# Memory queries by token halves at the start of layer two, and the first output step of the drain by token tile

## The chip, the cores and the metric

The kernel runs on one core of one Trainium2 chip. A core has five engines that run side by side, each with its own queue of instructions: TensorE (PE, matrix products, with its weight loads shown as PEld), VectorE (DVE), ScalarE (ACT), GpSimd (POOL) and SyncE (SP), which here only issues transfers. Times are microseconds (us) on the device, from the first to the last instruction of one execution and what lies around them; several executions are summed up by their median.

## The reference, cut to what matters

Two layers act on 1024 tokens of width 1024. Each layer projects its input x once into main columns, memory queries and two gates, runs a main branch and a cross-attention into 256 memory tokens, gates both, projects out and normalizes. The change lies where layer two (index 1) begins and where it ends.

```python
def memory_attention(q_mem, mem, w_mem_kv):
    mkv = mem @ w_mem_kv
    mk = mkv[..., :D_MEM].reshape(B, M, MEM_HEADS, MEM_HEAD_DIM)
    mv = mkv[..., D_MEM:].reshape(B, M, MEM_HEADS, MEM_HEAD_DIM)
    q = q_mem.reshape(B, S, MEM_HEADS, MEM_HEAD_DIM)
    logits = jnp.einsum('bshd,bmhd->bhsm', q, mk, ...) * (MEM_HEAD_DIM ** -0.5)
    p = jax.nn.softmax(logits, axis=-1)
    return jnp.einsum('bhsm,bmhd->bshd', p.astype(mv.dtype), mv).reshape(B, S, D_MEM)

def mixer_sublayer(x, mem, w_in, w_mem_kv, w_out, main_fn):
    h = x @ w_in
    ...
    y = jnp.concatenate([y_main * jax.nn.silu(g_main), y_mem * jax.nn.silu(g_mem)], axis=-1)
    return y @ w_out
...
        x = layer_norm(ALPHA * x + y, ln_g[layer], ln_b[layer])
```

D_MEM is 512: four heads of 128. The memory tokens and their keys and values don't depend on x. The memory queries do, and so wait in layer two for the normalized output of layer one.

## The kernel before

**Precision.** Every product is made of three matmuls. An operand is split into a high part (a copy rounded to fp32r, made by ACT at line 187) and a low part (the difference in bf16, made by DVE or POOL at line 188); the products high by high, high by low and low by high are added up in PSUM. `grouped` (line 220) puts the high by high products of a group first, or with `turned` last.

**A slab** (line 231) projects one block of 128 output columns for all 1024 tokens. It loads its weights in two pieces of 128x512 into `raw` (four buffers in a ring), splits each into the rings `w` and `wl` (four buffers each), and then makes two halves of 24 matmuls: first tokens 0 to 511, then tokens 512 to 1023. Each half fills one of the two banks of PSUM named `pj`, and at its end an evacuation empties the bank. The function is a generator: what calls it decides how far it runs. For a memory query the evacuation is one `hi_lo` (line 184), a copy on ACT and a difference on DVE.

**The seam between the layers.** `OutProj.rest` (line 532) ends layer one: for each pair of row tiles (256 tokens) it makes the output projection, and `norm` (line 565) adds the residual and normalizes on DVE with one square root on ACT. A normalized row tile becomes input of layer two in `turned_rows` (line 340): ACT and DVE make two half-precision parts (L344, L345), SP issues two transposing transfers (L347, L348), and ACT, DVE and POOL write the transposed block into the tensors called A (L349, L350, L351). For the last two row tiles (tokens 768 to 1023) this is called from `mem_attention` of layer two, through the list `turns`.

**Layer two begins** with `mem_kv(1)` (line 284), which loads and splits the memory tokens, then `mem_attention` (line 370): the two last row tiles, the four memory keys one after another (`keys`, 24 matmuls of 128x256 each, which need no x), and then the four memory queries as slabs, with the values of a head after each (the first value between the two halves of the first query). The split of a memory weight's first piece is given to POOL (line 301).

**Layer two ends** in `OutProj.early` (line 521), the first output step: product group 2 (the memory heads) for the first pair of row tiles, while the last heads of the main attention still run, pumped in small pieces between them. `open` (line 488) takes its four banks: two named `L` for the first row tile and the two `pj` for the second. `rest` then runs the other steps; that with product group 1 of the first pair needs the output of the last pair of heads, which `pair_out` (line 984) multiplies with its gate on POOL and writes to DRAM.

**What sets the order.** PE runs in the order in which the program is written. The instructions of ACT, DVE, POOL and SP are put in order when the program is built, by a planner that sees the whole program; on the chip each queue runs strictly in that order, so that one waiting instruction holds up all that stand behind it.

Of the kernel before, what the change touches and what calls it, by code (L numbers as in the profile page):

```python
# [9 lines left out]
F32 = mybir.dt.float32  # L10
F32R = mybir.dt.float32r
# [66 lines left out]
def run(units):  # L78
    for _ in units:
        pass  # L80
# [19 lines left out]
def trunk_kernel(ctx, tc, x, xT, memT, win, wk, wv0, wv, wmk, wmv, wout, poolw, pscale, lng, lnb, bforget, out):  # L100
# [25 lines left out]
    def sb(shape, tag, bufs, dt=F32, where=None):  # L126
        return (where or pool).tile(shape, dt, tag=tag, name=nm(tag), bufs=bufs)
# [4 lines left out]
    def G(shape=(P, S), dt=F32):  # L132
        return sb(list(shape), "G", 4, dt)
# [17 lines left out]
    def cut(pair, *key):  # L151

        return type(pair)(t[key] for t in pair)
# [5 lines left out]
    def in_place(make, shape):  # L159

        hi = make(list(shape))
        return hi, InPlace((make(list(shape), BF16), hi.bitcast(BF16)[..., 1::2]))
# [34 lines left out]
        nc.gpsimd.tensor_scalar(hi, src, 1.0, 1.0, ALU.mult, ALU.mult)  # L197
        nc.gpsimd.tensor_tensor(lo[0], src, hi.bitcast(F32), ALU.subtract)  # L198

    def split_w(src_dram, shape, by=nc.vector):  # L200
        r = raw(shape)
        nc.sync.dma_start(r, src_dram)
        h, l = in_place(wt, shape)
        gp_hi_lo(h, l, r) if low[0] else hi_lo(h, l, r, by=by)
        return h, l

# [21 lines left out]
        for i, (a, b) in enumerate(terms):  # L228
            nc.tensor.matmul(acc, a, b, start=i == 0, stop=i == len(terms) - 1)  # L229

    def slab(pieces_dram, XH, XL, evac, banks=("pj", 2)):

        ready = isinstance(pieces_dram, list)
        if ready:
            ws = pieces_dram
        else:
            ws = [split_w(pieces_dram[0], [P, 4, P])]
            yield 0
            ws.append(split_w(pieces_dram[1], [P, 4, P]))
            yield 0  # L240

        def terms(n, kts):
            cols = slice(n * NH, (n + 1) * NH)
            out = []
            for kt in kts:
                h, l = ws[kt // 4]
                out.append(three((h[:, kt % 4, :], cut(l, slice(None), kt % 4)), (XH[:, kt, cols], cut(XL, slice(None), kt, cols))))
            return out

        def put(acc, a, b, start, stop):  # L250
            nc.tensor.matmul(acc, a, b, start=start, stop=stop)  # L251
            since[0] += NH

        if ready:
            accs = [ps([P, NH], *banks) for _ in range(2)]
            for kt in range(KT):
                both = [terms(n, [kt])[0] for n in range(2)]
                for i in range(3):
                    for n in range(2):
                        put(accs[n], *both[n][i], kt == 0 and i == 0, kt == KT - 1 and i == 2)  # L260
                yield 6 * NH
            for n in range(2):
                evac(slice(n * NH, (n + 1) * NH), accs[n])
            return
        for n in range(2):
            acc = ps([P, NH], *banks)
            one, two = (terms(n, range(4 * pc, 4 * pc + 4)) for pc in range(2))
            order = grouped(one) + grouped(two, True) if n == 0 else grouped(two + one)
            if n:
                order = order[:KT] + order[KT + KT :] + order[KT : KT + KT]  # L270
            for j, (a, b) in enumerate(order):
                put(acc, a, b, j == 0, j == len(order) - 1)
                if j == len(order) - 1:
                    evac(slice(n * NH, (n + 1) * NH), acc)
                yield NH
# [93 lines left out]

    def mem_attention(l, XH, XL, kv, qtile, ytile, yd):  # L370

        (kh, kl, v, undo), keys, vals = kv
        qs = []
        if l:
            while turns:
                turns.pop(0)(lambda: vt([P, D], F16), lambda: vt([P, 2 * KT, P], F16))
            for h in range(4):
                keys(h)
        for h in range(MH):
            qh, ql = in_place(qtile, [P, S])  # L380
            units = slab(win[l, 8 + h], XH, XL, lambda cols, acc: hi_lo(qh[:, cols], cut(ql, slice(None), cols), acc))
            if l and not h:
                run(islice(units, 3 * KT + 2))
                vals(0)
            run(units)
            qs.append((qh, ql))
            if not l:
                keys(h)
            if not l or h:
                vals(h)  # L390
        ys, gs = [ytile() for _ in range(MH)], [G() for _ in range(MH)]
        pt, fill = {}, Fill()
        for h in range(MH):
# [58 lines left out]
    class OutProj:  # L452
# [68 lines left out]
        def early(self, y, yh, yl):  # L521


            nc.sync.dma_start(y, self.yd[2, :, :, : 2 * P])
            yield
            for two in (slice(0, 2), slice(2, 4)):
                hi_lo(yh[:, two, :], cut(yl, slice(None), two), y[:, two, :], True)
                yield
            self.accs = self.open(0)
            yield from self.products(self.accs, 2, yh, yl)  # L530

        def rest(self, resid, XH, XL, dst):
            self.split(24)
# [169 lines left out]
    with tc.tile_pool(name="in1", bufs=1) as in1:  # L703
# [7 lines left out]
        def vt(shape, dt=F32R):  # L711
            return sb(shape, "V", 4, dt, in1)

        kv = mem_kv(1)
        with tc.manual_schedule(engines={PE}):
            mem_attention(1, XH, XL, kv, xy, lambda: vt([P, S], F32), y1d[2])
        cumd = dram.tile([HEADS, S], F32, name="cumd")
        fg = G((P, 8, ST * HEADS))
        flog = fg[:, 0, :]
# [444 lines left out]
```

## Time and profile before

| | us |
|---|---|
| median of 3 runs | 1215.21 (1212.19 to 1216.25) |
| the profiled execution | 1217.81, of which its span is 1215.6 |
| PE busy | 1180.0 (97% of the span) |
| DVE busy | 798.4 (66%) |
| ACT busy | 616.6 (51%) |
| POOL busy | 200.4 (16%) |
| PE's last matmul of layer one | ends about 456.4 |
| last token of layer two's input written | 479.6 |
| last matmul | ends 1207.3 |

Times in the trace count from the span's start. A wait row names the waiting engine and line, what released it, and then the total, the number and the longest of such waits. A timeline row has start, duration, engine, line, operation, output and input tiles, and in brackets the idle time before it and what ended it. A row of windows gives, for a stretch, busy time and count of each engine, the granted clock of TensorE, and the share of the DMA engines. Two instructions that follow each other on an engine overlap a little in the records: copies of 128x512 on ACT last 0.62 us each and start 0.52 us apart.

### The profile page before, as it was taken

How to read it: one execution, taken by the hardware profiler on the slowest of the kernel's cores; microseconds unless marked ns; L12 is line 12 of the kernel's file. 1: busy time of each engine (PE TensorE's matmuls, PEld its weight loads, DVE VectorE, ACT ScalarE, POOL GpSimd, SP SyncE). 2: the span in 40 equal slices, each digit the busy share in tenths (PEclk: the TensorE clock that was granted, in tenths of full speed). 3: DMA queues.
4: the chain of work that ended last, by engine and by line, in shares of the span. 5: the costliest groups of instructions: out<-in, count | busy, mean ns of one | idle time of the engine just before them, and what ended most of it. 6: DMA issues, size and time to landing. Idle time of an engine off the chain costs nothing. (4 is left out here: it accounts for less than half of the span.)

```text
span 1215.6 us, 19488 instructions
## 1 busy us (share of the span) xinstructions
PE 1180.0 (97%) x6837; PEld 743.0 (61%) x6954; DVE 798.4 (66%) x1868; ACT 616.6 (51%) x1318; POOL 200.4 (16%) x304
## 2 busy tenths in 40 slices
PE   8999999999999997999999999999999999999997
PEld 4566665555555555666775666666666666655554
DVE  6644767375666657357555878777878878775654
ACT  6433654262522235356333777767766777783110
POOL 2000000000000012100003334333334324530000
PEclk9999999999999999999999999999999999999998
DMA  6333654242445567245527789889897999995431
GB/s 234 108 102 93 133 113 156 78 130 71 142 153 156 156 173 184 77 107 103 175 53 170 158 184 182 177 169 187 176 194 165 196 178 210 235 234 181 167 110 47
DMA packets 284305, 182.83 MB, mean 150 GB/s; under 512 B 229168, under 2 KB 242608, under 8 KB 284208
## 3 DMA queue, kind: packets, MB, share of 16 engines
q1 hardware_dynamic: 284208, 181.59, 61.4%
q8 instruction: 54, 0.88, 0.3%
q14 instruction: 43, 0.35, 0.1%
HBM read 94.97 MB, written 22.61 MB: 97 GB/s over the span
## 5 line engine op out<-in xcount | busy, mean ns | idle before, releaser
L251 PE MATMUL pj<-A,w 128*128 128x512 f32 (+1 forms) x1887 | 600.5, 399 | 3.6 <-ACT A L187 2.2
L251 PE MATMUL pj<-A,wl 128*128 128x512 bf16 x951 | 360.7, 381 | 4.8 <-DVE wl L188 0.6
L251 PEld LDWEIGHTS pj<-A,w 128*128 128x128 f32 x976 | 180.8, 189 | 45.7 <-ACT A L187 3.1
L251 PEld LDWEIGHTS <-w 128*128 128x128 bf16 x992 | 95.8, 98 | 123.3 <-issue 36.0
L251 PEld LDWEIGHTS <-wl 128*128 128x128 bf16 x992 | 97.5, 98 | 95.1 <-issue 5.8
L915 ACT ACTIVATE T<-MK,s 128x512 f32<-128x512 f32 x192 | 111.0, 578 | 58.0 <-DVE s L907 36.7
L937 DVE SCALAR_TENSOR_TENSOR P<-T,s,P 128x512 f16<-128x512 f32 x192 | 111.9, 613 | 31.5 <-ACT P L936 30.0
L936 ACT ACTIVATE P<-T,s 128x512 f16<-128x512 f32 x192 | 102.6, 575 | 48.7 <-issue 27.4
L518 PEld LDWEIGHTS <-T 128*128 128x128 bf16 x736 | 70.6, 98 | 87.3 <-issue 4.4
L188 DVE TENSOR_TENSOR wl<-raw,w 128x512 bf16<-128x512 f32 x98 | 69.2, 712 | 82.8 <-ACT w L187 81.4
L187 ACT CAST w<-raw 128x512 fp32r<-128x512 f32 x106 | 64.8, 617 | 98.5 <-PE pj L251 67.6
L229 PE MATMUL L<-B,B 128*128 128x512 f32 (+3 forms) x384 | 109.9, 389 | 3.2 <-DVE s L907 2.9
L229 PEld LDWEIGHTS L<-B,B 128*128 128x128 f32 x384 | 71.1, 189 | 28.5 <-DVE s L907 9.0
L351 POOL TENSOR_SCALAR A<-A 128x1024 bf16<-128x1024 f32 x8 | 8.4, 1052 | 423.5 <-ACT A L349 423.5
L907 DVE CUSTOM_DVE_ANT_0 MK<-L,R 128x512 f32<-128x512 f32 (+3 forms) x128 | 72.5, 567 | 8.4 <-DMA R<-cumd 5.0
L899 POOL TENSOR_SCALAR_AFFINE_SELECT R<-R 128x128 f32<-128x128 f32 x128 | 41.4, 329 | 207.8 <-DVE s L907 111.5
L198 POOL TENSOR_TENSOR wl<-raw,w 128x512 bf16<-128x512 f32 x54 | 69.1, 1280 | 3.5
L188 DVE TENSOR_TENSOR T<-T,T 128x1024 bf16<-128x1024 f32 x23 | 31.9, 1387 | 50.8 <-ACT T L187 50.7
L187 ACT CAST T<-T 128x1024 fp32r<-128x1024 f32 x23 | 24.1, 1048 | 76.9 <-DMA T<-y1d 50.4
L197 POOL TENSOR_SCALAR w<-raw 128x512 fp32r<-128x512 f32 x54 | 34.3, 634 | 74.8 <-PE pj L251 74.7
L518 PE MATMUL L<-B,T 128*128 128x512 bf16 (+1 forms) x164 | 43.0, 391 | 0.2
L966 PE MATMUL O<-T,V 128*128 128x128 f16 x576 | 38.5, 220 | 4.8 <-DMA T<-P 4.8
(277 smaller groups left out, 1744.1 us busy)
## 6 DMA issues: line engine op xcount, KB each, us to landing
raw<-in_win_dram SPq DMA_DIRECT2D x96, 256.0 KB, 2.9
raw<-in_wout_dram SPq DMA_DIRECT2D x40, 256.0 KB, 2.9
B<-B SPq DMA_DIRECT2D x32, 256.0 KB, 4.9
R<-cumd SPq DMA_DIRECT2D x16, 512.0 KB, 4.5
y0d<-Y SPq DMA_DIRECT2D x12, 512.0 KB, 3.2
T<-y0d SPq DMA_DIRECT2D x12, 512.0 KB, 5.3
T<-y1d SPq DMA_DIRECT2D x11, 512.0 KB, 4.2
raw<-in_wmk_dram SPq DMA_DIRECT2D x16, 256.0 KB, 2.7
```

The costliest lines, as they stand in the source:

```text
L187: pin(nc.scalar.copy(hi, src))
L188: pin(by.tensor_tensor(lo[0], src, hi.bitcast(F32), ALU.subtract))
L198: nc.gpsimd.tensor_tensor(lo[0], src, hi.bitcast(F32), ALU.subtract)
L229: nc.tensor.matmul(acc, a, b, start=i == 0, stop=i == len(terms) - 1)
L251: nc.tensor.matmul(acc, a, b, start=start, stop=stop)
L518: nc.tensor.matmul(acc, y, w, start=c == 2 and j == firsts[id(acc)], stop=c == 1 and j == lasts[id(acc)])
L899: nc.gpsimd.affine_select(R[:, qs], R[:, qs], [[-1, P]], ALU.is_ge, -NEG, base=0, channel_multiplier=1).ins
L907: nc.vector.tensor_tensor_reduce(p[:, lo:up], lg, R[:, lo:up], 1.0, top, ALU.add, ALU.min, m[:, n : n + 1])
L915: nc.scalar.activation(e, p[:, lo:up], AF.Exp, bias=top, scale=-1.0, accum_out=sums[:, n, hd % 2, i : i + 1],)
L936: nc.scalar.activation(pair[:, lo:up], e, AF.Copy, scale=r)
L937: nc.vector.scalar_tensor_tensor(pair[:, L + lo : L + up], e, r, pair[:, lo:up], ALU.mult, ALU.subtract)
L966: nc.tensor.matmul(acc[:, cols(i)], v[:, b, 2 * j : 2 * j + 2, :].rearrange("p e d -> p (e d)"), pt[hd, i][:, j, :], start=n == 0, stop=Fa ...
```

## The change

`split_w` and `slab` take an argument `make` that says where the split weights are kept. In layer two, `mem_attention` now builds the four memory queries first. The weights of the first two go to the rings `w` and `wl`, those of the last two to three buffers of the ring `P`, whose other use at that time is the weights and the two scale rows of layer one's output step. All eight pieces are loaded and split ahead of the last two row tiles; then come the first halves of all four queries; then `mem_kv(1)`, which was called ahead of `mem_attention` before; then the second halves in turn, with keys and values between them. In the drain, `early` orders its matmuls by row tile: all products of the first row tile (two banks), then those of the second with the high products last. The numbers of matmuls, splits and transfers stay as they were.

```diff
-    def split_w(src_dram, shape, by=nc.vector):
+    def split_w(src_dram, shape, by=nc.vector, make=wt):
         r = raw(shape)
         nc.sync.dma_start(r, src_dram)
-        h, l = in_place(wt, shape)
+        h, l = in_place(make, shape)
         gp_hi_lo(h, l, r) if low[0] else hi_lo(h, l, r, by=by)
...
-    def slab(pieces_dram, XH, XL, evac, banks=("pj", 2)):
+    def slab(pieces_dram, XH, XL, evac, banks=("pj", 2), make=wt):
...
-            ws = [split_w(pieces_dram[0], [P, 4, P])]
+            ws = [split_w(pieces_dram[0], [P, 4, P], make=make)]
             yield 0
-            ws.append(split_w(pieces_dram[1], [P, 4, P]))
+            ws.append(split_w(pieces_dram[1], [P, 4, P], make=make))
             yield 0
...
     def mem_attention(l, XH, XL, kv, qtile, ytile, yd):
 
-        (kh, kl, v, undo), keys, vals = kv
-        qs = []
+        qs = [in_place(qtile, [P, S]) for _ in range(MH)] if l else []
+
+        def query_units(h, make):
+            qh, ql = qs[h]
+            return slab(win[l, 8 + h], XH, XL, lambda cols, acc: hi_lo(qh[:, cols], cut(ql, slice(None), cols), acc), make=make)
+
+        def aside_homes():
+
+            lows = sb([P, 4, 4, P], "P", 4, BF16)
+            for n in range(2):
+                highs = sb([P, 2, 4, P], "P", 4, F32R)
+                left = [[highs[:, k], lows[:, 2 * n + k]] for k in range(2)]
+                yield lambda shape, dt=F32R, left=left: left[0].pop(0) if dt == F32R else left.pop(0)[0]
+
         if l:
+            homes = aside_homes()
+            units = [query_units(h, wt if h < 2 else next(homes)) for h in range(MH)]
+            for two in units:
+                run(islice(two, 2))
             while turns:
                 turns.pop(0)(lambda: vt([P, D], F16), lambda: vt([P, 2 * KT, P], F16))
-            for h in range(4):
+            for two in units:
+                run(islice(two, 3 * KT))
+            kv = mem_kv(l)
+        (kh, kl, v, undo), keys, vals = kv
+        for h in range(MH):
+            if l:
+                run(units[h])
+                for what, which in ((), ((keys, 0), (keys, 1)), ((keys, 2), (vals, 0)), ((keys, 3), (vals, 1)))[h]:
+                    what(which)
+            else:
+                qs.append(in_place(qtile, [P, S]))
+                run(query_units(h, wt))
                 keys(h)
-        for h in range(MH):
-            qh, ql = in_place(qtile, [P, S])
-            units = slab(win[l, 8 + h], XH, XL, lambda cols, acc: hi_lo(qh[:, cols], cut(ql, slice(None), cols), acc))
-            if l and not h:
-                run(islice(units, 3 * KT + 2))
-                vals(0)
-            run(units)
-            qs.append((qh, ql))
-            if not l:
-                keys(h)
-            if not l or h:
                 vals(h)
+        if l:
+            vals(2)
+            vals(3)
...
             self.accs = self.open(0)
-            yield from self.products(self.accs, 2, yh, yl)
+            parts = self.terms(self.accs, 2, yh, yl)
+            yield from self.ordered(grouped(parts[0] + parts[1]) + grouped(parts[2] + parts[3], True), 2)
...
-        kv = mem_kv(1)
         with tc.manual_schedule(engines={PE}):
-            mem_attention(1, XH, XL, kv, xy, lambda: vt([P, S], F32), y1d[2])
+            mem_attention(1, XH, XL, None, xy, lambda: vt([P, S], F32), y1d[2])
```

**PE at the seam.** First the order before, from the last matmul of layer one (bank L_3818) on; T are the split memory tokens, A the normalized input, w and wl the split weights.

```order
L518 MATMUL L_3818<-G_3128,T_3877 128x512
L229 LDWEIGHTS w_4104
L229 MATMUL pj_4101<-T_4051,w_4104 128x256
...
L229 MATMUL L_4141<-T_4050,w_4144 128x256 x4
...
L229 MATMUL L_4221<-T_4050,w_4224 128x256 x4
...
L251 MATMUL pj_4275<-A_3059,w_4265 128x512 x4
```

The same place in the changed kernel:

```order
L537 MATMUL L_3818<-G_3128,T_3877 128x512
L251 MATMUL pj_4123<-A_3059,w_4065 128x512 x4
...
L251 MATMUL pj_4150<-A_3059,w_4077 128x512 x4
...
L251 MATMUL pj_4177<-A_3059,P_4061 128x512 x4
...
L251 MATMUL pj_4204<-A_3059,P_4062 128x512 x4
...
L251 MATMUL pj_4260<-A_3059,w_4071 128x512 x4
```

The four keys (pj_4101 to L_4221) stood between layer one and the first product with A; now four half slabs on A, each in a new bank (pj_4123, 4150, 4177, 4204), follow at once, and pj_4260 is the first bank that takes tokens 512 to 1023.

**ACT at the seam, changed kernel**, from the half-precision part of row tile 6 (V_4103) to that of row tile 7 (V_4113) and on; P_4062 are the fourth query's weights, T_4231 and T_4233 memory tokens, B the queries.

```order
L344 ACTIVATE V_4103<-G_3998,unrow 128x1024
L187 CAST T_4231<-raw_4235 128x512
...
L349 ACTIVATE A_3059<-V_4107,unrow 128x8x128
L600 ACTIVATE s_4029<-s_4028 128x1
L187 CAST P_4062<-raw_4095 128x512
...
L187 CAST B_4052<-pj_4123 128x512
L187 CAST T_4233<-raw_4245 128x512
...
L344 ACTIVATE V_4113<-G_4020,unrow 128x1024
L187 CAST B_4054<-pj_4150 128x512
L349 ACTIVATE A_3059<-V_4117,unrow 128x8x128
L187 CAST B_4056<-pj_4177 128x512
```

The evacuations of the first three half slabs (B_4052, B_4054, B_4056) stand behind the row tiles' work on ACT. The order before at that place:

```order
L344 ACTIVATE V_4081<-G_3998,unrow 128x1024
L187 CAST w_4184<-raw_4182 128x512
L580 ACTIVATE s_4029<-s_4028 128x1
L187 CAST MK_4074<-pj_4101 128x256
...
L349 ACTIVATE A_3059<-V_4085,unrow 128x8x128
...
L187 CAST MK_4074<-L_4141 128x256
...
L344 ACTIVATE V_4091<-G_4020,unrow 128x1024
L187 CAST w_4265<-raw_4263 128x512
```

There the key evacuations (MK_4074) and the weights of keys and first query (w) stood between the same steps.

**PE in the drain.** Before, behind the first pieces of `early`; L_12359 is the second bank of the first row tile, pj_12360 and pj_12361 those of the second:

```order
L518 MATMUL L_12359<-V_11821,B_12019 128x512 x2
L518 MATMUL L_12359<-B_12200,B_12019 128x512 x2
L518 MATMUL pj_12360<-B_11717,B_12019 128x512 x2
L518 MATMUL pj_12360<-MK_11904,B_12019 128x512 x2
L518 MATMUL pj_12361<-V_11821,B_12019 128x512 x2
L518 MATMUL pj_12361<-B_12200,B_12019 128x512 x2
```

And in the changed kernel:

```order
L537 MATMUL L_12354<-V_11816,B_12014 128x512 x2
L537 MATMUL L_12354<-B_12195,B_12014 128x512 x2
L537 LDWEIGHTS B_12014
L537 MATMUL L_12353<-B_11713,B_12014 128x512
L537 LDWEIGHTS B_12015
L537 MATMUL L_12353<-B_11713,B_12015 128x512
```

The pj banks no longer come after the eight high products of the first row tile; the 16 small products of that row tile on the two L banks are now ahead of them.

## The prediction

> **What bounds the kernel now.** I read the first part of the page (busy times), then who waited for whom on PE, then the windows and timelines at the two places that the change touches. The page:
>
> ```profile
> PE 1180.0 (97%) x6837; PEld 743.0 (61%) x6954; DVE 798.4 (66%) x1868; ACT 616.6 (51%) x1318; POOL 200.4 (16%) x304
> ```
>
> PE is busy for 1180.0 of 1215.6 us, and the change leaves every matmul in place. So it can win only from the idle 35.6 us of PE, and only from waits that it takes away. PE's waits (total, number, longest):
>
> ```profile
> PE L L229 <- DVE s L907: 2.9, 8, 0.7
> PE pj L229 <- DVE T L188: 2.8, 1, 2.8
> PE pj L518 <- DVE G L282: 1.5, 1, 1.5
> PE pj L229 <- DVE wl L188: 1.1, 2, 0.8
> PE L L229 <- POOL wl L188: 0.9, 1, 0.9
> PE L L518 <- ACT T L187: 0.8, 1, 0.8
> PE pj L251 <- DVE wl L188: 0.6, 1, 0.6
> PE L L229 <- DVE wl L188: 0.4, 1, 0.4
> PE L L229 <- ACT w L187: 0.4, 1, 0.4
> ```
>
> The rows with T, w and wl at L229 and L251 are memory keys, a first value and a first query that wait for their split operands: 2.8 + 1.1 + 0.9 + 0.6 + 0.4 + 0.4 = **6.2 us**. The windows show that all of it lies at the seam:
>
> ```profile
> 456.40:460.10 3.70, 0.99 (x9) 0.73 (x8) 3.70 (x6) 3.60 (x6) 1.95 (x1) 1.00 0.10 18
> 460.10:480.00 19.90, 16.71 (x115) 12.36 (x116) 14.94 (x25) 10.44 (x21) 6.81 (x5) 1.00 0.95 227
> 500.00:530.00 30.00, 29.88 (x172) 19.86 (x173) 13.27 (x31) 9.19 (x16) 2.57 (x2) 1.00 0.29 87
> ```
>
> From 456.4 to 460.1 PE worked 0.99 of 3.70 us, and to 480.0 it worked 16.71 of 19.90; by 500 it is full. DVE and ACT were nearly full in the first stretch: memory splits, key weights and the normalization of the last row tiles shared them. The third row of the waits (1.5) is the second place, the first output step of the drain.
>
> **The change at the seam: what PE gets to do.** Instead of keys, PE now has four half slabs on tokens 0 to 511, which were written long before. Their length comes from the first query's second half, which began at 482.80, and the next half, which followed at 487.92 without a wait:
>
> ```profile
> 482.80 2.00 PE L251 MATMUL pj<-A,w 128*128 128x512 f32 x8
> 487.92 1.52 PE L251 MATMUL pj<-A,w 128*128 128x512 f32 x5
> ```
>
> That is 5.1 us, 5.2 with the change between the two kinds of matmul; four last 20.8 us, from 456.4 to **477.2**. Their weights: the first two loads take the place of the memory loads, whose first copy ran at 446.8, and the rest follow through the ring `raw` at 2.9 us a load:
>
> ```profile
> raw<-in_win_dram SPq DMA_DIRECT2D x96, 256.0 KB, 2.9
> ```
>
> With 0.62 for a copy and 0.68 for a low part, behind tile 6's and tile 7's normalization in DVE's new order, the first query's weights are split by 449, the second's by 456, the third's by 457, each ahead of its half (456.4, 461.6, 466.8).
>
> **What PE then waits for.** At 477.2 it needs tokens 512 to 1023, and so row tile 7. Before, that came so (ACT, DVE, SP, POOL):
>
> ```profile
> 446.82 0.62 ACT L187 CAST T<-raw 128x512 fp32r<-128x512 f32 x1 [1.90 <-DMA raw<-in_memT_dram]
> 459.11 1.15 ACT L344 ACTIVATE V<-G,unrow 128x1024 f16<-128x1024 f32 x1
> 467.44 1.15 ACT L349 ACTIVATE A<-V,unrow 128x1024 fp32r<-128x1024 f16 x1 [1.46 <-DMA V<-V]
> 471.97 1.15 ACT L344 ACTIVATE V<-G,unrow 128x1024 f16<-128x1024 f32 x1 [1.65 <-DVE G L588]
> 477.23 1.15 ACT L349 ACTIVATE A<-V,unrow 128x1024 fp32r<-128x1024 f16 x1 [0.90 <-DMA V<-V]
> 457.13 0.68 DVE L575 SCALAR_TENSOR_TENSOR G<-G,L 128x512 f32<-128x512 f32 x1
> 464.87 0.73 DVE L586 SCALAR_TENSOR_TENSOR G<-G,s,P 128x512 f32<-128x512 f32 x1
> 468.73 3.20 DVE L588 SCALAR_TENSOR_TENSOR G<-G,s,P 128x512 f32<-128x512 f32 x2
> 461.27 1.24 SPq L347 DMA_TRANSPOSE V<-V  x1
> 473.21 1.25 SPq L347 DMA_TRANSPOSE V<-V  x1
> 469.69 1.69 POOL L188 TENSOR_TENSOR wl<-raw,w 128x512 bf16<-128x512 f32 x1
> 478.46 1.10 POOL L351 TENSOR_SCALAR A<-A 128x1024 bf16<-128x1024 f32 x1 [1.07 <-ACT A L349]
> ```
>
> The first transfer of row tile 6 left at 461.27 and its user began at 467.44 (6.2 us); that of row tile 7 left at 473.21, its user at 477.23 (4.0). I step through the new order of ACT, DVE and SP with both prices, which are the ends of this unknown:
>
> 1. ACT's query weights are copied by about 453, so V of tile 6 waits only for layer one's last weights: 456.4, done 457.5; its transfer leaves at 457.6 (3.7 earlier than before) and lands at 461.6 or 463.8.
> 2. ACT then writes A (1.15), takes the square root of tile 7 (0.2), copies the fourth query's weights (two, 1.1) and empties the first query's bank (0.6): 464.6 or 466.8. DVE's part of that bank, behind two low parts, ends near 465.9 or 467.8. The third half slab takes this bank at 466.8: a wait of 0 or 1.0.
> 3. DVE scales tile 7 (L588, two halves at 0.73): 467.3 or 469.2. Before, it ended at 471.9, with 3.20 for the two, while POOL split a key weight (469.69, 1.69) beside it. That POOL work is now later.
> 4. The last memory pieces load behind the fourth query's low parts (+2.9), four copies follow on ACT (2.1), then V of tile 7 (1.15): done at 470.6 or 472.6. This, not the scaling, is what is late next. The second query's bank is emptied behind it, at 472.5 or 474.5; the fourth half, due at 472.0, waits 0.5 or 2.5.
> 5. The transfer takes 4.0 or 6.2, A 1.15: 475.8 or 480.0 (478.4 before).
>
> These waits do not add up to more than the last of them: PE goes on with the second halves at the later of the fourth half's end (472.5 or 474.5, plus 5.2, so 477.7 or 479.7) and the arrival of the third bank and of the tokens (about 476.5, or 481.0 with DVE's part of that bank). Against 477.2 it has lost **0.5 or 3.8**. I take 1.9, a little under the middle, because the transfers of tile 7 leave with as little beside them as before, when they took 4.0.
>
> [...]
>
> **The second halves** (20.8 us) alternate with four keys and four values. A key's weights now take `w` buffers that the first two queries give back only after their second halves. One key lasts 2.7 us, as the second before shows, from its first matmul to the next key's:
>
> ```profile
> 462.13 1.25 PE L229 MATMUL L<-T,w 128*128 128x256 f32 x9
> 464.85 0.27 PE L229 MATMUL pj<-T,w 128*128 128x256 bf16 x1
> ```
>
> There is at least one such product between each release and the use, and a split needs 2.3 (a copy 0.62, POOL's low part 1.69). Before, four keys back to back did wait there, but with the normalization on the same engines; at 500 to 530 PE was 29.88 of 30.00 busy with that spacing. I charge nothing; if this cover fails it costs 0.4 to 0.9 a piece, as the rows above, for the three last products 2 us.
>
> **The change in the drain: nothing.** The third wait row is the second row tile's bank, which was emptied late:
>
> ```profile
> 1079.92 0.67 DVE L282 SCALAR_TENSOR_TENSOR G<-G,pj 128x512 f32<-128x512 f32 x1
> 1080.65 0.74 PE L518 MATMUL pj<-V,B 128*128 128x512 f32 x2 [1.47 <-DVE G L282]
> 1088.41 0.47 PE L972 MATMUL O<-T,V 128*64 128x128 f16 x10
> 1096.68 0.68 ACT L978 ACTIVATE G<-O,unscale 64x512 f32<-64x512 f32 x1
> 1076.04 0.86 PE O L972 x26
> 1100.19 4.28 DMA y1d<-G
> 1104.56 6.15 DMA T<-y1d
> 1111.82 2.11 PE L L518 x8
> ```
>
> With 16 more matmuls of the first row tile ahead, some 3.5 us, the bank is free when it is asked for, and the 1.47 go. But the next thing that ends late is the last pair of heads: PE ends its product at 1088.9, ACT takes it only at 1096.68, behind weight copies that wait for loads, and then it goes through DRAM (the DMA rows, from the chain of waits) to PE at 1111.82. Between 1076.9 (the row O L972 x26) and there that chain has no piece of PE. PE already waited 0.8 there (the row with ACT T). None of ACT's order in this stretch is moved, and its copies wait for `raw` loads and for DVE. So PE comes 1.47 earlier to 1111.82 and waits 2.3 instead of 0.8. Gain 0; at most 1.5, if that chain follows PE after all.
>
> **Sum.** 6.2 − 1.9 = 4.3 at the seam, 0 in the drain: span 1215.6 to 1211.3. The profiled execution lasted 1217.81, 2.2 around its span, and lies 2.6 above the median 1215.21; the median goes to **1210.9**. Bounds: 6.2 − 0.5 + 1.5 = 7.2 better at best, and 6.2 − 3.8 − 2 = 0.4 at worst by these rows.
>
> **Rivals.** No change means within 0.3% (3.65 us), about what a measurement of this kernel can tell; the three runs shown span 4.06.
>
> - *The drain passes its gain on*: 4.3 + 1.5 = 5.8, 1209.4. For it: the 1.47 is a true stall of PE. Against: the chain of waits, as above. 0.13.
> [...]
> - *Slower: the ring `raw`.* Twelve loads share four buffers ahead of tile 7's transfers on SP's queue, and each waits for a DVE split which waits for row tile work. If the transfers stood behind a further turn (load 2.9, copies and splits 2.7) and took 6.2, tokens would come at 480.0 + 5.6 = 485.6, and a third turn would bring 491.2: 14 lost instead of 6.2, time 1223. It decides from 477.2 + 6.2 + 3.65 = 487.0 on. Against: one turn is counted in step 4 already. 0.09.
>
> The forecast itself has 0.50. Faster is forecast and first rival, 0.63; same 0.28; slower 0.09. The range takes in the best bound and the no change case: 1207.5 to 1215.5; the forecast's own is 1209 to 1211.5.
>
> **What would show it.** Right: at the seam no wait over 2.5 us, the first wait on L251 for a bank (B, ACT or DVE at L187 or L188) or for A; rows of L229 gone from PE's waits; the row pj L518 for DVE G gone and that of L L518 for ACT T grown to 2.3. Wrong: second halves starting after 481 (tiles late), waits at L229 after 500 (weights late), or the ACT T row still at 0.8 with the drain shorter.

## The result, and the profile after

The changed kernel took 1209.54 us (median of 7 runs, 1206.99 to 1211.75) and the kernel before, beside it, 1213.48 (7 runs, 1211.97 to 1216.25): a ratio of 0.9962, interval 0.9946 to 0.9978. In a later set on one chip with three other kernels the same change took 1207.24 (5 runs) against 1213.85 (14 runs): 0.9947, interval 0.9933 to 0.9961. So it is faster by 3.9 and by 6.6 us. In the first set the two executions with a mean granted clock of 0.998 took 1206.99 and 1207.95, and the five with 0.996 or 0.997 took 1208.03 to 1211.75; why that set's median is 2.3 us above the second's is not shown beyond that. The profiled execution of the first set lasted 1210.54 with a span of 1208.6; that of the kernel before had 1215.6.

The busy times, first part of the page, show that PE does the same work in less time:

```profile
PE 1178.9 (98%) x6837; PEld 743.2 (61%) x6954; DVE 795.9 (66%) x1868; ACT 616.0 (51%) x1318; POOL 199.7 (17%) x304
```

PE's waits after the change, as in the table of before:

```profile
PE O L985 <- DMA T<-P: 4.5, 6, 1.6
PE L L229 <- DVE s L926: 3.9, 10, 0.9
PE L L537 <- ACT T L187: 2.1, 1, 2.1
PE pj L251 <- ACT A L187: 1.2, 1, 1.2
PE pj L251 <- issue: 0.5, 3, 0.2
PE pj L251 <- POOL A L192: 0.3, 1, 0.3
```

All six rows that made up the 6.2 us (T, w and wl, at L229 and L251) are gone, and nothing has come in their place: the row with ACT A L187 belongs to the start of layer one, not to the seam. The bank wait of the drain (DVE G L282, 1.5) is gone too, and the wait for the last pair of heads (ACT T L187) has grown from 0.8 to 2.1. The windows at the two places (engine columns as before, the granted clock third from the end):

```profile
456.40:477.20 20.80, 20.69 (x94) 11.89 (x94) 13.16 (x25) 11.05 (x18) 2.50 (x2) 1.00 0.76 171
500.00:530.00 30.00, 29.86 (x207) 23.00 (x209) 18.44 (x54) 17.06 (x40) 5.13 (x4) 1.00 0.45 125
1101.00:1103.10 2.10, 0.02 (x1) 0.00 (x0) 0.00 (x0) 1.04 (x1) 0.00 (x0) 1.00 0.88 288
1103.10:1107.10 4.00, 3.95 (x10) 3.12 (x11) 2.64 (x2) 2.05 (x2) 0.00 (x0) 0.57 0.40 129
```

At the seam PE is busy for 20.69 of 20.80 us; the kernel before had 0.99 of 3.70 and then 16.71 of 19.90 there. The last row is the surprise. After the wait in the drain, PE was granted 0.57 of its clock for 4.0 us, which is 4.0 x 0.43 = 1.7 us lost behind a wait of 2.1. The timeline shows it as slower matmuls, 1.05 us for two:

```profile
1103.15 0.85 PE L537 MATMUL L<-R,T 128*128 128x512 f32 x2 [2.12 <-ACT T L187]
1103.80 1.05 PE L537 MATMUL L<-P,T 128*128 128x512 f32 x2
```

The same pair of matmuls in the second set's execution, after a shorter wait, lasts 0.62:

```profile
1101.51 0.73 PE L537 MATMUL L<-R,T 128*128 128x512 f32 x2 [0.94 <-ACT T L187]
1102.08 0.62 PE L537 MATMUL L<-P,T 128*128 128x512 f32 x2
```

To place the gain I read two starts off each PE timeline, layer two's first matmul and the drain's first output matmul, and take the rest from the span (us; each row is one profiled execution):

```text
                                      layer two  from there   from there
                                      begins     to drain     to the end
before                                456.35     616.94       142.31
the full change                       454.89     610.32       143.39
the full change, second set           455.44     609.24       140.62
seam part alone                       455.47     609.88       140.35
drain part alone                      454.99     615.92       141.29
full, late group order                455.41     609.37       140.22
full, late group order, second set    454.50     610.17       139.33
seam part, late group order           455.38     609.53       140.99
seam part, late group order, again    454.70     609.97       141.23
full, zero matmuls in the drain       455.19     608.79       141.42
three halves ahead                    455.34     611.03       139.53
four low parts on POOL                456.30     613.78       140.22
two halves ahead                      455.50     618.99       144.31
two halves ahead, zero matmuls        454.86     616.82       139.42
```

The first column is not the change's doing. Before and the POOL kernel begin layer two late, at 456.3, and both also lost clock at the start of layer one (0.50 from 8.0 to 11.4 us in before, a mean of 0.64 from 8 to 12 us in the POOL kernel); so 1.46 of the 7.0 us between the spans of the first two rows lie ahead of the change. The middle column is the seam's account: 616.94 and 615.92 with the old seam, 608.8 to 610.3 with the new one in the eight rows whose seam is that of the full change. From the first row to the second it is 6.6 us, the 6.2 of the wait rows and a little more. The last column is the drain's. The new order there has 1.0 less with the old seam (142.31 to 141.29); with the new seam it has 0.3 more (140.35 to 140.62), and 3.0 more in the execution whose clock fell, of which the fall is 1.7.

### The profile page after: what moved, and what is told of

It is laid out like the page before. It is cut to its first block, busy times and chain, and to the rows that moved or that the text cites. A ratio compares the mean times of both kernels' runs of the same rounds, so it can differ in the third digit from the quotient of the medians.

```text
span 1208.6 us, 19479 instructions
## 1 busy us (share of the span) xinstructions
PE 1178.9 (98%) x6837; PEld 743.2 (61%) x6954; DVE 795.9 (66%) x1868; ACT 616.0 (51%) x1318; POOL 199.7 (17%) x304
## 5 line engine op out<-in xcount | busy, mean ns | idle before, releaser
L251 PE MATMUL pj<-A,w 128*128 128x512 bf16 (+1 forms) x1826 | 580.8, 398 | 2.9 <-ACT A L187 1.2
L251 PE MATMUL pj<-A,wl 128*128 128x512 bf16 x919 | 347.5, 379 | 4.5 <-issue 0.5
L251 PEld LDWEIGHTS pj<-A,w 128*128 128x128 f32 x944 | 174.7, 188 | 44.0 <-ACT A L187 2.2
L251 PEld LDWEIGHTS <-w 128*128 128x128 bf16 x960 | 92.7, 98 | 119.1 <-issue 34.8
L251 PEld LDWEIGHTS <-wl 128*128 128x128 bf16 x960 | 94.3, 98 | 90.9 <-issue 6.0
L537 PEld LDWEIGHTS <-T 128*128 128x128 bf16 x736 | 70.6, 98 | 87.3 <-issue 4.7
L229 PE MATMUL L<-B,B 128*128 128x512 f32 (+3 forms) x384 | 110.1, 389 | 4.2 <-DVE s L926 3.9
L187 ACT CAST w<-raw 128x512 fp32r<-128x512 f32 x102 | 62.5, 618 | 86.9 <-PE pj L251 61.1
L229 PEld LDWEIGHTS L<-B,B 128*128 128x128 f32 x384 | 70.8, 189 | 30.0 <-DVE s L926 10.5
L187 ACT CAST T<-T 128x1024 fp32r<-128x1024 f32 x23 | 24.1, 1048 | 74.8 <-DMA T<-y1d 49.4
L537 PE MATMUL L<-B,T 128*128 128x512 bf16 (+1 forms) x163 | 43.2, 393 | 0.3
```

The source lines that it names most:

```text
L187: pin(nc.scalar.copy(hi, src))
L537: nc.tensor.matmul(acc, y, w, start=c == 2 and j == firsts[id(acc)], stop=c == 1 and j == lasts[id(acc)])
```

## The experiments

**Two theories.** *Theory A*: the seam wins all 6.2 us, since no part of the new work at the seam makes PE wait; in the drain the new order exchanges a wait for a bank for a longer one for the last pair, behind which the clock can fall, and so gives 1 to 2 us back. *Theory B*, the prediction's account: the seam wins about 4.3, the drain nothing.

**The seam part alone.** `early` gets its old order back:

```diff
-            parts = self.terms(self.accs, 2, yh, yl)
-            yield from self.ordered(grouped(parts[0] + parts[1]) + grouped(parts[2] + parts[3], True), 2)
+            yield from self.products(self.accs, 2, yh, yl)
```

> The change at the seam alone; the first output step of the drain is ordered as before. Theory A: the seam wins the whole 6.2 us of its waits, and the drain's new order gives back 1.5 to 2 us, because its wait for the last pair of heads grows from 0.8 to 2.1 us and the granted clock falls behind it. Then this kernel is 5.5 to 6.5 us faster than before (ratio about 0.995) and faster than the full change; PE waits 1.5 for the bank and about 0.8 for the last pair, with a granted clock of 1.0 behind that. Theory B: the seam wins about 4 us and the drain nothing, and this kernel is as fast as the full change (ratio 0.9965).

Measured: 1208.04 against 1214.32 (17 runs of the kernel before, shared by this set of four), ratio 0.9952 (0.9939 to 0.9965). One row of PE's waits answers to the drain:

```profile
PE pj L537 <- DVE G L282: 0.8, 1, 0.8
```

The bank wait is there, no wait for the last pair follows, and the time is 6.3 us below. That is the whole of 6.2, which speaks for A at the seam.

**The drain part alone.** The kernel before, with the new order in `early`.

> The drain's new order alone; the seam as before. Theory A: the bank's wait of 1.5 us is gone, the wait for the last pair is 2.1 to 2.3 us, and the clock granted in the 4 us behind it is near 0.57; the time is 0 to 2 us above before (ratio 1.000 to 1.0015), and the waits at the seam are still 6.2 us. Theory B: same waits, clock stays at 1.0, ratio 1.000.

Measured: 1214.67 against 1214.32, ratio 1.0006 (0.9998 to 1.0014). Two rows of PE's waits, and one of the windows at the old seam:

```profile
PE pj L229 <- ACT V L344: 2.2, 1, 2.2
PE L L518 <- ACT T L187: 1.6, 1, 1.6
```

```profile
460.00:464.00 4.00, 4.00 (x27) 3.80 (x27) 3.96 (x9) 2.01 (x5) 1.29 (x1) 0.67 1.14 233
```

The bank wait is gone, the last pair's wait has doubled from 0.8 to 1.6 (theory A had 2.1 to 2.3) and the time is unchanged: nothing is gained in the drain. Here the clock did not fall behind that wait but behind the old seam's wait of 2.2 us, which ended at 458.19: its mean is 0.67 from 460 to 464. So the old seam, too, can pay more than its waits.

**The late group order.** Each entry of the list below is a pair of row tiles and a product group. The step of the second pair of row tiles with product group 0 is taken ahead of the first pair's last step, so that PE has work while the last pair of heads arrives:

```diff
-                accs[0], order = self.accs, [(0, 0), (1, 2), (0, 1), (1, 0), (1, 1)]
+                accs[0], order = self.accs, [(0, 0), (1, 2), (1, 0), (0, 1), (1, 1)]
```

> The full change, and in the drain the second pair of row tiles also takes product group 0 before the first pair takes group 1, the one that needs the last pair of heads: 48 matmuls, some 10.5 us, are put ahead of the wait. Theory A: the wait of 2.1 us is gone and the clock stays at 1.0 there, so 3 to 4 us are won against the full change (ratio to before 0.993 to 0.994). Theory B (the clock does not matter): 2.1 us, ratio 0.9945. Against both: the second pair's bank (O) or the banks of the third pair come late, and nothing is won.

Measured: 1206.31, ratio 0.9934 (0.9922 to 0.9946), with no row for ACT T L187 at L537: the fastest version of this set. Theory A had 0.993 to 0.994 here, 3 to 4 us below the full change. Against the full change's second measurement, 0.9947, 0.0013 or 1.6 us is left of that.

**Zero matmuls in the drain's wait.** Nine matmuls with a zero matrix, added to a bank that is open, ahead of the step that waits:

```diff
+                if self.accs and (sp, c) == (0, 1):
+                    for _ in range(9):
+                        nc.tensor.matmul(accs[1][1][1], nought, self.ws[1][4][1][0][0], start=False, stop=False)
```

> The full change with nine matmuls of a zero operand (about 1.95 us) put directly ahead of the step that waits for the last pair of heads; they add zeros to an open bank. PE is busy while it waits, and nothing else is moved. Theory A: the step starts when it did, its wait is about 0.2 us, the granted clock behind it stays at 1.0, and 1.0 to 1.7 us are won against the full change. Theory B: no change against the full change, or 0.1 to 0.3 us slower.

Measured: 1207.48, ratio 0.9946 (0.9934 to 0.9958). Two rows of its timeline:

```profile
1099.69 2.11 PE L584 MATMUL O<-V,nought 128*128 128x512 bf16 x9
1101.45 0.82 PE L539 MATMUL L<-R,T 128*128 128x512 f32 x2
```

No wait and no slow matmuls follow. Whether that is a gain can't be read from its time: its interval overlaps those of the full change and of the seam part alone.

**The full change again, and the seam part alone in the late group order**, on one chip, with the next two kernels.

> The full change, unaltered, beside the three other kernels on one chip. Theory A (the seam wins all 6.2 us that PE waited there; the new order in the drain trades a bank wait of 0.8 to 1.5 for a longer wait on the last pair's weights, behind which the granted clock can fall, and so gives back 1 to 2 us): ratio to the kernel before about 0.996, 4 to 5 us faster, and 1 to 1.5 us slower than the seam part alone with the late group order. Theory B (seam about 4.3, drain 0): ratio 0.9965, and the same time, within 0.5 us, as the seam part alone with the late group order. In its waits: a row L537 <- ACT T L187 of 1.6 to 2.3 us, none at L251 above 1.2.

Measured: 1207.24 against 1213.85 (14 runs, shared by this set), ratio 0.9947 (0.9933 to 0.9961), and 0.9 us of wait for the last pair.

> The change at the seam alone, with the old order of the first output step, and with the second row tile's product group 0 ahead of the first row tile's last step (order 0-0, 1-2, 1-0, 0-1, 1-1). It has the bank wait of before and no wait for the last pair. Theory A: the row for DVE G L282 of 0.8 to 1.5 us is back, there is no L537 <- ACT T row, and the time is 1.0 to 1.5 us above that of the full change with the same group order, which had ratio 0.9934: so about 0.9945. If the bank wait is hidden even so (rival: the work behind it only shifts), the ratio is 0.9934 as well, and the drain's edit is worth nothing by any order.

Measured: 1207.01, ratio 0.9947 (0.9934 to 0.9960). Its waits have the bank row back:

```profile
PE pj L537 <- DVE G L282: 1.5, 1, 1.5
```

This kernel came out at its forecast of 0.9945. But the full change is as fast, where theory A had it 1 to 1.5 us slower. So the drain's half of theory A falls: the new order doesn't give 1 to 2 us back as a rule, and the fall in clock of the first profiled execution isn't part of every one. The two kernels differ in two edits, so they don't price either one alone. The seam's half stands: 6.6 and 6.8 us.

**Three halves ahead instead of four.**

```diff
-            for two in units:
+            for two in units[:3]:
                 run(islice(two, 3 * KT))
```

> The full change, but only the first three queries' first halves stand ahead of the memory tokens' weights and the second halves, instead of four; the fourth's comes right before its second half. Margin theory: in the full change the last tokens are written 20.4 us after layer one's last matmul and PE asks for them at 20.8, so with three halves (15.6) PE waits 4.5 to 5 us on L251 for A, and the time is 4.5 us above the full change's (ratio 0.9995 to 1.0005). Rival (the fourth half gives no cover, since a bank or a query weight holds PE or the row tiles come earlier with one evacuation less ahead of them on ACT and DVE): a wait of 1.5 to 3.5 us and the time 1 to 3 us above.

Measured: 1208.37, ratio 0.9964 (0.9949 to 0.9978), 1.1 us above the full change. Three rows of its timeline, ACT, PE and POOL:

```profile
472.00 1.15 ACT L349 ACTIVATE A<-V,unrow 128x1024 fp32r<-128x1024 f16 x1 [3.66 <-DMA V<-V]
473.20 2.35 PE L251 MATMUL pj<-A,w 128*128 128x512 f32 x9 [1.55 <-ACT A L349]
473.23 1.04 POOL L351 TENSOR_SCALAR A<-A 128x1024 bf16<-128x1024 f32 x1 [10.26 <-ACT A L349]
```

PE waits 1.55, not 4.5 to 5: the margin theory's account was wrong, and the sizes are the rival's. Three things make up the 3.2 between them. PE starts at 473.20, when ACT has written the high part of the last tokens; POOL's low part is only begun then. The second half's first matmuls are the high by high ones (`grouped`), which last 2.35 us, so the low part isn't asked for until 475.38. In the full change the high part is there 1.35 ahead of the low. Next, three halves lasted 16.3 us, to 471.65, rather than 15.6. And the high part came 17.8 us after layer two's start, 1.2 sooner than in the full change, mostly because tile 7's first transfer took 3.9 us and not 4.9. What the fourth half covers is the high part; the low part has two microseconds more.

**The low parts on POOL.** The four low parts of the third and fourth query's weights are made by POOL:

```diff
-            return slab(win[l, 8 + h], XH, XL, lambda cols, acc: hi_lo(...), make=make)
+            return slab(win[l, 8 + h], XH, XL, lambda cols, acc: hi_lo(...), make=make, by=nc.vector if make is wt else nc.gpsimd)
```

> The full change, with the four low parts of the third and fourth query's weights made by POOL instead of DVE (1.69 us each on POOL against 0.68 on DVE). Port theory (POOL's splits stretch DVE's instructions with two inputs, as in the row of 3.20 us of the kernel before): DVE's scaling rows of row tile 7 stand beside those splits and grow from 2 x 0.73 to 2.5 us or more, the last tokens come 1.5 to 3 us later, PE waits 1 to 2.5 us on L251 ahead of the first query's second half or for the fourth query's weights, and the time is 1 to 2.5 us above the full change's. Rival (DVE has four operations of 0.68 less ahead of the scaling, and POOL's splits lie elsewhere): tokens come 1 to 2 us earlier, no new wait, the time the same within 0.5 us.

Measured: 1210.88 (11 runs), ratio 0.9979 (0.9970 to 0.9988), 3.6 us above the full change. Its timeline, POOL, DVE, PE, and its windows behind the wait:

```profile
465.46 2.67 POOL L188 TENSOR_TENSOR P<-raw,P 128x512 bf16<-128x512 f32 x2
466.17 0.75 DVE L604 TENSOR_TENSOR s<-s,s 128x1 f32<-128x1 f32 x1
466.96 2.39 DVE L608 SCALAR_TENSOR_TENSOR G<-G,s,P 128x512 f32<-128x512 f32 x2
469.27 0.68 DVE L188 TENSOR_TENSOR B<-pj,B 128x512 bf16<-128x512 f32 x1
470.00 12.22 PE L251 MATMUL pj<-A,P 128*128 128x512 f32 x47 [2.71 <-DVE B L188]
```

```profile
470.00:474.00 4.00, 4.00 (x11) 2.08 (x12) 2.94 (x4) 2.04 (x4) 0.00 (x0) 0.59 0.84 227
```

In the change itself L608 lasts 1.41 and L604 0.15 (its timeline, below, has the first). Beside POOL's splits they take 2.39 and 0.75. The evacuation of the first query's bank (B) stands behind them and ends at 469.95, so the third half starts 2.71 late, and the clock then has a mean of 0.59 over four microseconds: 2.71 + 4.0 x 0.41 = 4.4 us. The table has 613.78 − 609.24 = 4.5 more between seam and drain than the full change beside it. The stretch that the first theory named is shown, but it is 1.6 of the 2.71, and the wait came at the third half rather than the second halves. The same trace shows two other differences that can make up the rest; how it divides between them is not shown. In the change itself the low part of B stands ahead of L608 in DVE's order (464.53 below); here the planner put it behind. And ACT copied that bank at 465.67, 9.4 us after layer two's start instead of 8.1.

**A long wait made on purpose, without and with zero matmuls in it.** Two halves ahead (`units[:2]`), and the same with 28 zero matmuls ahead of the first query's second half:

```diff
+                for i in range(zeros):
+                    nc.tensor.matmul(acc, nought, terms(0, [0])[0][1][1], start=i == 0, stop=i == zeros - 1)
```

> The full change with only the first two queries' first halves ahead of the second halves, to make one long wait on purpose. With three ahead PE waited 1.55 us for the high part of the last tokens; with two it gets there 5.2 us earlier, so the wait is 6 to 6.8 us. Clock theory (what a wait costs is its length and, behind a long one, some 4 us at a granted clock near 0.6, another 1.7 us): windows behind the wait show a clock of 0.55 to 0.9 for about 4 us, and the time is 5.2 + 1.7, so near 6.9 us above three ahead (which was 1.1 above the full change): close to the kernel before, ratio 1.0005 to 1.002. Rival (a wait costs its length only): clock 1.00 behind it, ratio near 0.9995 and 1.7 us less.

Measured: 1217.40 (12 runs) against 1214.90 (23 runs, shared by this set), ratio 1.0024 (1.0013 to 1.0035). That is 0.0060 above three halves ahead, some 7.3 us: the clock theory had 6.9, its rival 5.2. From its timeline and its windows:

```profile
474.10 4.23 PE L251 MATMUL pj<-A,w 128*128 128x512 f32 x9 [7.61 <-ACT A L349]
```

```profile
466.00:468.00 2.00, 0.49 (x3) 0.05 (x1) 2.00 (x4) 1.09 (x3) 0.00 (x0) 1.00 0.83 294
468.00:472.00 4.00, 0.00 (x0) 0.00 (x0) 2.58 (x4) 1.15 (x2) 0.00 (x0) 0.56 0.98 236
474.00:478.30 4.30, 4.20 (x10) 2.83 (x11) 0.28 (x1) 0.05 (x1) 1.05 (x1) 0.50 0.08 29
```

> The kernel with two first halves ahead, and 28 matmuls with a zero matrix (6.0 us) put into the wait, whose result is overwritten: they add work that nothing needs. Clock theory: the wait left is under 1 us, the clock stays at 1.00, and the time is 1.2 to 2 us below that of the same kernel without them, though it has 6 us more of PE work. Rival (a wait costs its length only): the same time within 0.4 us, or slower, where the zeros outlast the wait.

Measured: 1213.93 (11 runs), ratio 0.9994 (0.9985 to 1.0003), from its timeline:

```profile
465.69 6.22 PE L274 MATMUL pj<-A,nought 128*128 128x512 bf16 x28
473.53 2.34 PE L253 MATMUL pj<-A,w 128*128 128x512 f32 x9 [1.62 <-ACT A L353]
```

Both begin the last tokens' matmuls nearly 8 us after the end of the second half slab, when ACT has written A; but the nine matmuls that follow last 4.23 us after an idle PE and 2.34 after one that multiplied zeros. The kernel with 6.2 us more of work is 3.5 us faster, and the two intervals don't overlap. The wait left was 1.6, not under 1. Of the 3.5, 1.9 are these nine matmuls; the rest isn't placed. Over whole executions the mean granted clock was 0.990 to 0.996 in all twelve without the zeros, and 0.998 or 0.999 in ten of the eleven with them. The profiled execution of the kernel without zeros also fell in clock in the drain, behind 2.3 us of wait for the last pair, and is its slowest; how often its others fell there is not known.

**The late group order once more, with and without the drain's edit.**

> The full change with the late group order, once more, on one chip with the seam part alone in that order. If the drain's edit is worth the bank wait (0.8 to 1.5 us in the kernels that have it) once no wait for the last pair follows: 0.8 to 1.5 us below the seam part alone in that order. If it is worth nothing by any order: the same within 0.4 us. In the earlier two sets this kernel was 8.0 us and that one 6.8 us below the kernel before.

> The change at the seam alone with the late group order, once more, beside the full change with that order. A row for DVE G L282 of 0.8 to 1.5 us. Ratio 0.994 to 0.995; by the theory that the drain's edit is worth its wait, 0.8 to 1.5 us above the full change with that order, by its rival the same.

Measured: with the edit 1206.54 (6 runs), ratio 0.9933 (0.9919 to 0.9947); without it 1207.41 (5 runs), 0.9940 (0.9926 to 0.9954). The difference is 0.9 here. Over both sets it is 1206.31 (11 runs) against 1207.20 (10 runs), also 0.9, and the table's last column has 140.22 and 139.33 with the edit, 140.99 and 141.23 without. All point to the edit being worth some 0.9, most of the bank wait of 1.5, once a later step no longer waits; the intervals overlap, so it is likely rather than shown. This version, the full change with that order, is the fastest of all, 8 us below the kernel before. (The 609.97 in the middle column of the last kernel without the edit contains a fall in clock at 827 us, of which more at the end.)

## Why the prediction was right, and where its steps were off

The prediction said 1210.9, faster by 4.3; measured were 3.9 and 6.6. Its forecast, that the keys' waits go and the second halves come early enough, is what happened. One term of the sum was mis-sized: the **loss of 1.9** that it drew from its five steps ("I take 1.9, a little under the middle"), which was 0. That the first set's 3.9 lies so near 4.3 is luck: in its two profiled executions the seam won 6.6, and the drain gave 1.1 back through a fall in clock that the prediction didn't have. The rows of the changed kernel's timeline, with ACT, DVE, SP, POOL and PE, show where:

```profile
454.42 1.15 ACT L344 ACTIVATE V<-G,unrow 128x1024 f16<-128x1024 f32 x1 [3.15 <-PE L L537]
455.59 1.24 SPq L347 DMA_TRANSPOSE V<-V  x1
458.66 0.69 DVE L188 TENSOR_TENSOR T<-raw,T 128x512 bf16<-128x512 f32 x1 [0.89 <-ACT T L187]
459.38 1.50 SPq L289 DMA_DIRECT2D raw<-in_memT_dram  x2
460.36 1.15 ACT L349 ACTIVATE A<-V,unrow 128x1024 fp32r<-128x1024 f16 x1
461.91 1.19 DVE L350 TENSOR_SCALAR A<-V,unrow 128x1024 bf16<-128x1024 f16 x1
463.86 0.68 DVE L188 TENSOR_TENSOR P<-raw,P 128x512 bf16<-128x512 f32 x1
464.53 0.68 DVE L188 TENSOR_TENSOR B<-pj,B 128x512 bf16<-128x512 f32 x1
465.13 1.41 DVE L608 SCALAR_TENSOR_TENSOR G<-G,s,P 128x512 f32<-128x512 f32 x2
465.72 10.79 PE L251 MATMUL pj<-A,P 128*128 128x512 f32 x47
466.57 1.15 ACT L344 ACTIVATE V<-G,unrow 128x1024 f16<-128x1024 f32 x1 [0.92 <-DVE G L608]
467.93 2.74 SPq L347 DMA_TRANSPOSE V<-V  x1
472.78 1.15 ACT L349 ACTIVATE A<-V,unrow 128x1024 fp32r<-128x1024 f16 x1 [4.59 <-DMA V<-V]
473.89 0.48 DVE L350 TENSOR_SCALAR A<-V,unrow 128x1024 bf16<-128x1024 f16 x1 [4.26 <-DMA V<-V]
474.01 1.27 POOL L351 TENSOR_SCALAR A<-A 128x1024 bf16<-128x1024 f32 x1 [11.19 <-ACT A L349]
476.36 2.23 PE L251 MATMUL pj<-A,w 128*128 128x512 f32 x9
```

Layer two begins at 454.89 in this execution, 1.46 earlier than in that of before; times below count from there, and the prediction's from its 456.4.

1. *Row tile 6.* Its transfer left at 455.59 and ACT took its result at 460.36 without having to wait, so it lasted 4.8 at most; that of tile 7, for which ACT did wait, took from 467.93 to 472.78, 4.9. Both lie between the two prices of 4.0 and 6.2. Right.
2. *The first bank.* It is emptied by 465.2, 10.3 in; the third half asks for it at 465.72, 10.8 in, since a half lasts 5.4 and not 5.2. No wait, with 0.5 to spare. The kernel with the low parts on POOL, where it was emptied 13.7 in, is what that margin looks like when it fails.
3. *Scaling of row tile 7 beside less POOL work.* 1.41 for two, as forecast from 0.73 each instead of 3.20. That POOL was the cause is shown by that same kernel, which has 2.39 beside POOL's splits; by what mechanism POOL's work stretches DVE's is not shown. Beside POOL's work on A of tile 6 it was L350 that grew, 1.19 against 0.48 for tile 7, and PE didn't wait for it.
4. *The last memory pieces* were to load behind the fourth query's low parts (+2.9) and hold V of tile 7 to 14.2 or 16.2. **This step failed**: the loads left at 459.38, well ahead of those low parts (the last at 463.86). The first of them left 0.03 after the low part of the first memory piece ended (458.66 + 0.69), so by the timing the last pieces took the buffers of the first memory pieces, and not those of the fourth query's weights. The copies were not late, and V waited for the scaling alone, the very thing that the step had said would not be late. It was done at 467.7, 12.8 in.
5. *The tokens* were expected at 19.4 or 23.6. Their high part was there at 473.9, 19.0 in, and the low at 20.4. PE asked at 476.36, 21.5 in, where the prediction had 20.8 for the four halves, and it asked for the low part only some 2 us later, as the kernel with three halves showed. The prediction let PE wait for all of A; it needs the high part first.

*The second halves* were charged nothing, and the rows of L229 for split operands are indeed gone; 500 to 530 is 29.86 busy of 30.00.

*The drain* was charged nothing, and what was measured agrees with that (1.0006 alone; with the new seam 0.9962 and 0.9947, beside 0.9952 for the seam part alone). The rows came as said: the bank wait went, the last pair's grew to 2.1 of the 2.3 forecast in one execution and 0.9 in the other. What was missed is that a wait can have a second price, the clock behind it: a mean of 0.57 over 4.0 us behind the 2.1, and 1.00 behind the 0.9. That the pair's arrival was fixed was too strong: ACT took the product at 1096.68 before and at 1087.75 after, 8.9 earlier with PE only 8.1 earlier.

```profile
1087.75 0.68 ACT L997 ACTIVATE G<-O,unscale 64x512 f32<-64x512 f32 x1
1102.05 1.04 ACT L187 CAST T<-T 128x1024 fp32r<-128x1024 f32 x1 [8.63 <-DMA T<-y1d]
```

*The rivals.* The case of no change (0.28) needed new waits at the seam, and there was none at L251. The ring `raw` didn't turn again. The gain that the second set measured (6.6) is over the forecast's best bound for the seam, 6.2 − 0.5, and not because the drain passed its 1.5 on: the seam lost nothing. The 0.4 above the 6.2 of the wait rows isn't placed.

## What to carry to other kernels

Where an engine waits at a seam between two stages, put ahead of it the work that depends only on what has long been written, and count the cover against the first operand that is asked for: with products split into high and low parts, ordered high first, the low part may come two microseconds later (2.2 in the kernel with three halves). A margin at such a place is easily spent: four splits moved to POOL cost 3.6 us, in part by DVE's instructions that they stretched (L608 took 2.39 and not 1.41) and in part by the clock behind the wait (a mean of 0.59 over 4.0 us). And a wait on PE can have a second price: behind those of 2.1 to 2.7 us at these two places a lower clock followed in four profiles, at a cost of some 1.7 us each, and in that of before it did not. Work of no use put into the wait can be cheaper than the wait: with 6.2 us of zero matmuls in it, the kernel that otherwise waited 7.6 was 3.5 us faster.

## What the runs showed of the hardware

The granted clock fell behind waits of 2.1 us (drain, full change), 2.2 (old seam, drain part alone), 2.3 (drain, two halves), 2.7 (POOL kernel) and 7.6 (two halves). It did not behind 2.7 at the old seam of the first profile of before (clock 1.00 in the windows that the prediction shows), nor behind the waits of 1.8 and less in the middle and the drain of these kernels, but for one: in the seam part alone with the late group order, the second time, it fell at 827.1 (worked out from the mean of 0.89 from 824 to 828). PE was idle for 1.97 of the eight microseconds from 820 to 828, and the longest wait of that kernel, for a transfer, was 1.8.

```profile
PE O L984 <- DMA T<-P: 4.9, 6, 1.8
820.00:824.00 4.00, 3.48 (x30) 2.47 (x29) 3.42 (x14) 3.27 (x9) 0.54 (x2) 1.00 1.08 264
824.00:828.00 4.00, 2.55 (x35) 1.87 (x35) 2.06 (x9) 2.58 (x9) 0.29 (x1) 0.89 1.13 251
828.00:832.00 4.00, 4.00 (x14) 1.95 (x14) 3.52 (x9) 2.65 (x6) 0.29 (x1) 0.69 1.07 225
```

At the start of layer one, where PE begins to work and waits for its first tokens, it also fell behind 2.2 (before), 1.5 (two halves) and 1.4 (POOL kernel), and did not behind 1.2 or 1.0 (the full change). In windows of 0.2 us the falls of before and of the full change are a clock of 0.50, from 7.98 to 11.39 and from 1103.61 to 1107.02: 3.41 us each, so a cost of up to 3.41 x 0.50 = 1.7 us. The windows of four microseconds of the other short falls lose 1.7 as well (1.68 to 1.72), and those of the long wait 5.1, three times as much: 0.50 for some 10.2 us. The 0.57 to 0.67 above are means over four microseconds that hold such a fall in part. Where the wait's start can be told, the fall came 2.0 to 3.2 us after it, sometimes when PE was at work again, as at 459.2 in the drain part alone (wait from 456.03 to 458.19). In the long wait it came while PE was still idle: 466 to 468 has 1.00 and 468 to 472 has 0.56, so about 2 us after the last matmul at 466.5.

What sets off a fall is not shown: 2.7 us of wait were followed by one in the POOL kernel and not in before, and the shortest waits here with a fall are 1.4 at the start and 1.8 or less later. That zero matmuls in the wait kept the clock up was measured: it was 1.00 from 466 to 482 with them and 0.50 from 472 to 478.3 without, and nine matmuls took 2.34 against 4.23.

On ACT a step that waits held up what stood behind it: in the changed kernel L349 waited 4.59 us for its transfer, and the copy of the third bank behind it started at 473.83, some 2.7 us after the third half slab ended (465.72 + 5.4).
